# Row products with an operand in PSUM and every second low part on GpSimd, in a hybrid attention and expert block

## The chip, the cores and the metric

One core of a Trainium2 chip runs the whole kernel. The metric is device time in microseconds, median of three runs.

## The reference

One residual layer over 512 tokens of width 2048, and a last RMSNorm. The first half is a mixer of two attentions (eight heads each), gated and merged. The change lies in the second half, a product-key retrieval of single-neuron experts:

```python
def peer_ffn(h, w_query, sub_keys, expert_u, expert_v):       # h: RMSNorm(x), 512 x 2048
    q = (ht @ w_query).reshape(n_tok, 8, 2, 128)
    scores = einsum('thpc,hpnc->thpn', q, sub_keys)           # 128 keys per half
    # top 16 of each half, top 16 of the 16x16 sums: 128 experts of 16384 per token
    gates = softmax(top_score)
    act = gelu(einsum('thkd,td->thk', expert_u[ids], x))
    return einsum('thk,thkd->td', gates * act, expert_v[ids])
```

All arrays are float32, and the output must agree to nearly that.

## The kernel before, in words

Activations lie with the features on partitions (16 blocks of 128) and tokens along the row. To keep precision at the fast rate, each matmul operand is split into a rounded high part and the low part that is left, and `mm3` (L115 to L118) multiplies high with high, high with low and low with high. Weights come through `wload` (L95): a block of 128x2048 in two halves of 128x1024 (512 KB each, on SP's queue); ScalarE makes the high part (`wh`, L108), VectorE subtracts it for the low part (`wl`, L109). There are three buffers each of `wh` and `wl`, and four of the raw halves.

The expert stage begins at L487. Query projections, keys and scores give each token its 128 experts (`choose`, L653: tops, indices, gates). Then two ways of computing the experts run side by side:

- Densely, for the first 352 tokens (`TD`): for each of 128 blocks of 128 experts, `expert_up` (L532) multiplies all of them with the tokens (`psu`), VectorE scales (L536), ScalarE applies gelu. 54 of these blocks (`NS`) are done early: 40 beside `choose`, five after each head, and 14 beside the scatter (L777 to L793), which spreads the gates into a dense table in DRAM (`gsp`, stored from GpSimd's queue). Their activations are kept in DRAM (`gact_sp`). The rest are computed between the product groups.
- By gathered rows, for the last 160 tokens: GpSimd gathers for each of them the row of one expert (128 rows of 2048, 1 MB, `row_of`, L557), and VectorE multiplies it: an up product with the token's own row (L568, L577) that sums into one number, or a down product that adds the weighted row to an accumulator (L586, L597). There are 320 of them: 128 and 32 up, 128 and 32 down, in the list `todo` (L613). `pace` (L549) takes them from the list as the dense work goes on: 0.8 for each block in the early stage, then at a rate that empties the list at the end. The 32 tokens of the second kind stand four times side by side, so that 32 rounds serve their 128 experts. `token_rows` (L514) turns token columns into rows through TensorE transposes; `back` and `back_b` (L599, L606) turn the sums back.

The dense products come in 16 groups of eight expert blocks (L828). `weigh` (L808) brings the next activation, loads a group's gates when its first block comes (`gg`, which lies in columns of h2 that the dense part doesn't use, in one copy), multiplies (L817), and splits the result into high (L820) and low (L821): `wg`, nine buffers. Activations pass through four buffers (`gl`). Then 16 accumulations of 24 matmuls (`psy`), each added to the residual by VectorE (L841).

PSUM: two banks `pu`, two `py`, two `psx` and two `pg` in the first part of the stage; the last four give way to two `py2`, so that `psy` turns over four banks. Row buffers: two in the early stage, a third (`ex`) for every third row from the product groups on.

The order within each engine's queue is not the order of the program text: a scheduler fills each queue with what is ready first by its own estimate, earlier text first among the ready, and each queue then runs strictly in order. `tc.issue_after` holds an instruction behind a named one on its engine.

Of the kernel before, what the change touches and what calls it, by code (L numbers as in the profile page):

```python
# [13 lines left out]
ALU = mybir.AluOpType  # L14
# [36 lines left out]
def block_kernel(ctx, tc, xT, gains, w_vf, bf, w_qk, w_v, w_g, w_br, w_o, w_q, keysT, uT, vP, expert_u, expert_v, outT):  # L51
# [450 lines left out]
    rows_p = pool("rows", 1)  # L502
    accg = acc[:, :, T - P:]
    def norm2():
        ps = py.tile([P, T], F32, tag="py", name="psn2")
        nc.tensor.matmul(ps, ones, rstd, start=True, stop=True)
        rsqrt(rstd, ps, [gl.tile([P, T], F32, tag="gl", name="rs2") for i in range(3)])
        pt = py.tile([P, NT, P], F32, tag="py", name="psrt")
        for t in range(NT):
            nc.tensor.transpose(pt[:, t], rstd[:, t * P:(t + 1) * P], ident)  # L510
        for t in range(NT):
            nc.vector.tensor_copy(rstd_t[:, t:t + 1], pt[:, t, 0:1])

    def token_rows(cols, dst, x_dst=None):  # L514

        for j in range(0, KC, 4):
            if x_dst is not None:
                ps = py.tile([P, 4, P], F32, tag="py", name="psxg")
                for i in range(4):
                    nc.tensor.transpose(ps[:, i], cols(j + i), ident)  # L520
            ph = py.tile([P, 4, P], F32, tag="py", name="pshg")
            for i in range(4):
                tmp = gl.tile([P, P], F32, tag="gl", name="tmp")
                src = cols(j + i)
                nc.vector.tensor_scalar(tmp if len(src.shape) == 2 else tmp.rearrange("p (g m) -> p g m", m=MB), src,
                                        g_sb[:, KC + j + i:KC + j + i + 1], None, op0=ALU.mult)
                nc.tensor.transpose(ph[:, i], tmp, ident)
            if x_dst is not None:
                nc.scalar.activation(x_dst[:, j:j + 4], ps, AF.Copy)
            nc.scalar.activation(dst[:, j:j + 4], ph, AF.Copy)  # L530
# [15 lines left out]
    accb = h2g  # L546
    count, extra = [0], []
# [9 lines left out]
    def row_of(table, ids, i):  # L557
        count[0] += 1
        third = extra and count[0] % 3 == 0
        row = (extra[0] if third else rows_p).tile([P, KC, P], F32, tag="row", bufs=1 if third else 2, name="row")  # L560
        nc.gpsimd.indirect_dma_start(out=row.rearrange("p k q -> p (k q)"), out_offset=None, in_=table,  # L561
                                     in_offset=bass.IndirectOffsetOnAxis(ap=ids[:, i:i + 1], axis=0))
        return row

    def gather_up(i, after):
        row = row_of(expert_u, idx, i)
        with tc.issue_after(after):
            nc.vector.scalar_tensor_tensor(row, row, rstd_t[:, NT - 1:NT], h2g, op0=ALU.mult, op1=ALU.mult,  # L568
                                           accum_out=gact[:, i:i + 1])

    def rows_b(i, after):
        token_rows(lambda k: acc[:, k, TD:TD + MB].unsqueeze(1).to_broadcast([P, GB, MB]), h2g)

    def gather_up_b(i, after):
        row = row_of(expert_u, idx_b, i)
        with tc.issue_after(after):
            nc.vector.scalar_tensor_tensor(row, row, rstd_b, h2g, op0=ALU.mult, op1=ALU.mult,  # L577
                                           accum_out=gact_b[:, i:i + 1])

    def gather_down(i, after):  # L580
# [3 lines left out]
        row = row_of(expert_v, idx, i)  # L584
        with tc.issue_after(after):
            nc.vector.scalar_tensor_tensor(accg, row, gact[:, i:i + 1], accg, op0=ALU.mult, op1=ALU.add)  # L586

    def gather_down_b(i, after):
# [3 lines left out]
        row = row_of(expert_v, idx_b, i)  # L592
        with tc.issue_after(after):
            if i == 0:
                nc.vector.tensor_scalar(accb, row, gact_b[:, :1], None, op0=ALU.mult)
            else:
                nc.vector.scalar_tensor_tensor(accb, row, gact_b[:, i:i + 1], accb, op0=ALU.mult, op1=ALU.add)  # L597
# [8 lines left out]
    def back_b(i, after):  # L606
        for j in range(0, KC, 4):
            ps = py.tile([P, 4, MB], F32, tag="py", name="psbackb")
            for i in range(4):
                nc.tensor.matmul(ps[:, i], accb[:, j + i], sel_b, start=True, stop=True)  # L610
# [4 lines left out]
    todo += [(gather_down_b, i) for i in range(SB)] + [(lambda i, after: None, 0), (back, 0), (back_b, 0)]  # L615
# [12 lines left out]
    with ExitStack() as s1:  # L628
# [3 lines left out]
        psx = pool("psx", 2, space=PSUM, cm=s1)  # L632
        pg = pool("pg", 2, space=PSUM, cm=s1)
# [83 lines left out]
        for h in range(NH):  # L717
            sc = []
            sv = se.tile([P, 2, HT, NK], F32, tag="sv", name="sv")
            for p in range(2):  # L720
# [3 lines left out]
                if b == 3:  # L724
                    token_rows(lambda k: acc[:, k, T - P:], h2g, accg)
# [6 lines left out]
                ps = psx.tile([P, NT, NK], F32, tag="psx", name="pss")  # L732
# [16 lines left out]
        ps = psx.tile([P, T], F32, tag="psx", name="psrep")  # L749
# [18 lines left out]
        for n, src in enumerate((ia, ib, gt)):  # L768
            ps = psx.tile([P, ND, P], F32, tag="psx", name="pstr")
# [7 lines left out]
        for tb in range(TD // TB):  # L777
            st = se.tile([P, NK, TB], F32, tag="st", name="st")
            for t4 in range(0, TB, 4):
# [4 lines left out]
                ps = pg.tile([P, 4, NK], F32, tag="pg", name="psgt")  # L784
# [11 lines left out]
    extra.append(ex)  # L796
# [7 lines left out]


    ahead = []

    def weigh(n):  # L808
# [14 lines left out]

    ws = [weigh(0)]
    assert len(started) == NS
    rate[0] = len(todo) / (2 * NK - NS - 8)
    py2 = pool("py2", 2, space=PSUM)
    for grp in range(NG):  # L828
        while len(ws) < GC:
            ws.append(weigh(grp * GC + len(ws)))  # L830
        for jb in range(KC // JJ):
            w = wload(vP[grp, jb])
            for jj in range(JJ):
                j = jb * JJ + jj
                ps = (py, py2)[j % 2].tile([P, T], F32, tag="py", name="psy")
# [7 lines left out]
        ws = []  # L843
# [4 lines left out]
    fin = [rows_p.tile([P, 4, T], F32, tag="row", bufs=2, name="fin") for i in range(2)]  # L848
# [78 lines left out]
```

## Time and profile before

| | us |
|---|---|
| median of 3 runs (3779.3 to 3790.0) | 3787.84 |
| profiled execution | 3782.03 |
| its span | 3780.3 |

| 40 slices of 94.5 us | busy tenths of VectorE |
|---|---|
| slices 1 to 14 (attention, mixer, output) | 3 to 5 |
| slices 15 to 17 (query projection) | 4, 6, 7 |
| slices 18 to 40 (experts) | 5 to 9, mostly 8 |

The profile is one execution. Busy times of matmuls overlap, so a busy TensorE is not one at its peak: the number of matmuls in a stretch says more. GpSimd's busy time counts gathers only for as long as it writes their descriptors; the transfer comes after.

### The profile page before, as it was taken

Reading aid. Unit: us, or ns where it says so; the run is one execution under the profiler, and the core shown is the slowest. Engines: PE = TensorE matmul, PEld = TensorE weight load, DVE = VectorE, ACT = ScalarE, POOL = GpSimd, SP = SyncE. Lnnn points to the kernel's source line nnn. Section 1 sums busy time; section 2 is a strip of 40 time slices with the busy share of each in tenths; the row PEclk is TensorE's granted clock in tenths of the full one; section 3 lists DMA queues with packets and bytes.
Section 4 is the critical chain, followed back from the end, with each engine's and each line's share of the span. In section 5 each row is a group of like instructions: output and inputs, shape, how many; then the busy total and the mean of one; then the engine's idle time right before and its main releaser. Section 6 shows DMA issues by size and latency. Waiting matters only on the chain.

```text
span 3780.3 us, 52236 instructions
## 1 busy us (share of the span) xinstructions
PE 3676.0 (97%) x20745; PEld 3384.4 (90%) x20745; DVE 2640.2 (70%) x4067; ACT 1291.3 (34%) x1808; POOL 515.2 (14%) x432
## 2 busy tenths in 40 slices
PE   8999999999999999999999898999999999999997
PEld 7888888888887878799999798999999999999997
DVE  5333445444555346799699888988888888888885
ACT  4334222232223223344355332333333333333333
POOL 0000000000000000011211122222222222222220
PEclk9999999999999999999999999999999999999999
DMA  4222222222224233376867899998999989999983
GB/s 141 80 78 77 98 95 95 89 87 84 85 95 138 95 100 101 128 267 251 294 229 264 288 336 333 352 334 326 333 336 348 345 324 349 340 343 344 332 306 112
DMA packets 233701, 827.26 MB, mean 219 GB/s; under 512 B 21736, under 2 KB 82664, under 8 KB 189680
## 3 DMA queue, kind: packets, MB, share of 16 engines
q1 hardware_dynamic: 174032, 450.30, 34.5%
q0 software_dynamic: 49920, 360.74, 24.8%
q10 hardware_dynamic: 9504, 12.88, 0.9%
q8 instruction: 163, 2.67, 0.3%
q14 instruction: 82, 0.67, 0.1%
HBM read 784.72 MB, written 39.11 MB: 218 GB/s over the span
## 4 chain that ended last, share of the span: by engine, by line
PE 81%; DVE 9%; DMA 5%; issue 3%; ACT 1%; SPq 0%; POOL 0%; DVEq 0%; POOLq 0%; ACTq 0%
PE psy L118 7%; PE psy L117 7%; PE psy L116 7%; PE psu L118 6%; PE psu L116 6%; PE psu L117 6%; PE psg L118 3%; PE psg L117 3%; PE psq L118 3%; PE psg L116 3%; PE psq L117 3%; PE psq L116 3%; DVE wl L109 2%; DVE ab L787 2%; PE psk L118 2%
## 5 line engine op out<-in xcount | busy, mean ns | idle before, releaser
L108 ACT ACTIVATE wh<-wr 128x1024 fp32r<-128x1024 f32 x768 | 813.6, 1061 | 1933.4 <-PE psy L117 581.0
L109 DVE TENSOR_TENSOR wl<-wr,wh 128x1024 fp32r<-128x1024 f32 x768 | 935.5, 1221 | 504.4 <-ACT wh L108 500.5
L116 PE MATMUL psy<-wg,wh 128*128 128x352 f32 x2048 | 668.6, 327 | 26.6 <-ACT wg L820 25.8
L117 PE MATMUL psy<-wg,wh 128*128 128x352 f32 x2048 | 672.0, 328 | 8.7 <-DVE wg L821 8.7
L118 PE MATMUL psu<-h,wl 128*128 128x352 f32 x2048 | 666.7, 326 | 12.8 <-DVE wl L109 12.5
L118 PE MATMUL psy<-wg,wl 128*128 128x352 f32 x2048 | 669.8, 328 | 8.4 <-DVE wl L109 8.3
L116 PE MATMUL psu<-h,wh 128*128 128x352 f32 x2048 | 666.6, 325 | 4.0 <-DVE gl L536 2.9
L117 PE MATMUL psu<-h,wh 128*128 128x352 f32 x2048 | 662.8, 324 | 0.0
L116 PEld LDWEIGHTS psy<-wg,wh 128*128 128x128 f32 x2048 | 391.1, 191 | 29.0 <-ACT wg L820 27.6
L118 PEld LDWEIGHTS psu<-h,wl 128*128 128x128 f32 x2048 | 385.5, 188 | 18.9 <-DVE wl L109 18.7
L117 PEld LDWEIGHTS psy<-wg,wh 128*128 128x128 f32 x2048 | 391.0, 191 | 11.0 <-DVE wg L821 10.9
L118 PEld LDWEIGHTS psy<-wg,wl 128*128 128x128 f32 x2048 | 391.0, 191 | 10.0 <-DVE wl L109 9.9
L116 PEld LDWEIGHTS psu<-h,wh 128*128 128x128 f32 x2048 | 386.6, 189 | 5.0 <-issue 3.2
L117 PEld LDWEIGHTS psu<-h,wh 128*128 128x128 f32 x2048 | 386.9, 189 | 0.0
L561 POOL DMA_INDIRECT row<-eu,idx x128 | 192.4, 1503 | 901.5 <-DVE row L568 606.4
L568 DVE SCALAR_TENSOR_TENSOR row<-row,rstd_t,h2g 128x2048 f32<-128x2048 f32 x128 | 300.1, 2345 | 6.5 <-DMA row<-eu,idx 6.5
L586 DVE SCALAR_TENSOR_TENSOR acc<-row,gact,acc 128x2048 f32<-128x2048 f32 x128 | 300.1, 2345 | 1.9 <-DMA row<-ev,idx 1.9
L561 POOL DMA_INDIRECT row<-ev,idx x128 | 182.2, 1424 | 508.0 <-DVE acc L586 478.1
L116 PE MATMUL psq<-h,wh 128*128 128x512 f32 x512 | 204.5, 399 | 8.8 <-ACT wh L108 8.8
L117 PE MATMUL psq<-h,wh 128*128 128x512 f32 x512 | 205.6, 401 | 1.5 <-DVE h L167 1.4
L118 PE MATMUL psq<-h,wl 128*128 128x512 f32 x512 | 204.6, 400 | 0.1
L118 PE MATMUL psg<-h,wl 128*128 128x512 f32 x512 | 203.3, 397 | 0.0
(311 smaller groups left out, 5513.7 us busy)
## 6 DMA issues: line engine op xcount, KB each, us to landing
wr<-uT SPq DMA_DIRECT2D x256, 512.0 KB
wr<-vP SPq DMA_DIRECT2D x256, 512.0 KB
wr<-w_qk SPq DMA_DIRECT2D x64, 512.0 KB
wr<-w_g SPq DMA_DIRECT2D x64, 512.0 KB
gsp<-st POOLq DMA_DIRECT2D x22, 1024.0 KB
wr<-w_br SPq DMA_DIRECT2D x32, 512.0 KB
wr<-w_o SPq DMA_DIRECT2D x32, 512.0 KB
wr<-w_q SPq DMA_DIRECT2D x32, 512.0 KB
```

The source lines that it names most:

```text
L108: nc.scalar.activation(hi, raw, AF.Copy)
L109: ins = nc.vector.tensor_tensor(lo, raw, hi.bitcast(F32), op=ALU.subtract)
L116: nc.tensor.matmul(ps, wh, ah, start=start, stop=False)
L117: nc.tensor.matmul(ps, wh, al, start=False, stop=False)
L118: nc.tensor.matmul(ps, wl, ah, start=False, stop=stop)
L561: nc.gpsimd.indirect_dma_start(out=row.rearrange("p k q -> p (k q)"), out_offset=None, in_=table, in_offset=bass.IndirectOffsetOnAxis(ap=i ...
L568: nc.vector.scalar_tensor_tensor(row, row, rstd_t[:, NT - 1:NT], h2g, op0=ALU.mult, op1=ALU.mult, accum_out=gact[:, i:i + 1])
L586: nc.vector.scalar_tensor_tensor(accg, row, gact[:, i:i + 1], accg, op0=ALU.mult, op1=ALU.add)
L787: nc.vector.tensor_scalar(ab[0][:, i], i128, tr[0][:, t:t + 1], tr[2][:, t:t + 1], op0=ALU.is_equal, op1=ALU.mult)
```

## The change

- `wload`: from the expert stage on, the low part of the second half of each block is subtracted on GpSimd.
- The operand that a row product reads or accumulates into lies in PSUM: one tile of four banks (`pr`), which holds in turn norm2's work, the token rows, and the sums. `token_rows` transposes into it without a copy, and no longer turns the residual itself. The down products start from the first weighted row, and `back` adds the finished sums to the residual; ScalarE copies them out of PSUM (`sums`). `back` now comes before the down products of the second kind.
- Three row buffers in one pool throughout.
- PSUM: `pu` two banks, `px` two banks for all else (scores, scatter, `psy`, backs), `pr` four.
- The gates of the next group are asked for after the second weight block of a group, its first activation is weighed after the seventh.

```diff
@@ wload
-            ins = nc.vector.tensor_tensor(lo, raw, hi.bitcast(F32), op=ALU.subtract)
+            second = more and s == 1
+            ins = (nc.gpsimd if second else nc.vector).tensor_tensor(lo, raw, hi.bitcast(F32), op=ALU.subtract)
@@ pools
-    py = pool("py", 2, space=PSUM)
+    px = pool("px", 2, space=PSUM)
+    pr = pool("pr", 1, space=PSUM)
-    h2g = gpool.tile([P, KC, P], F32, name="h2g")
-    rows_p = pool("rows", 1)
-    accg = acc[:, :, T - P:]
+    rows_p = pool("rows", 3)
+    held = [None]
+    def hold(name):
+        held[0] = pr.tile([P, KC, P], F32, tag="pr", name=name)
+        return held[0]
@@ token_rows
-    def token_rows(cols, dst, x_dst=None):
...
+    def token_rows(cols, name):
+        dst = hold(name)
+        for j in range(KC):
+            tmp = gl.tile([P, P], F32, tag="gl", name="tmp")
+            src = cols(j)
+            nc.vector.tensor_scalar(tmp if len(src.shape) == 2 else tmp.rearrange("p (g m) -> p g m", m=MB), src,
+                                    g_sb[:, KC + j:KC + j + 1], None, op0=ALU.mult)
+            nc.tensor.transpose(dst[:, j], tmp, ident)
@@ row products
-            nc.vector.scalar_tensor_tensor(row, row, rstd_t[:, NT - 1:NT], h2g, op0=ALU.mult, op1=ALU.mult,
+            nc.vector.scalar_tensor_tensor(row, row, rstd_t[:, NT - 1:NT], held[0], op0=ALU.mult, op1=ALU.mult,
                                            accum_out=gact[:, i:i + 1])
...
+    def add_row(row, g, i, ins):
+        with tc.issue_after(ins):
+            if i == 0:
+                nc.vector.tensor_scalar(hold("accg"), row, g[:, :1], None, op0=ALU.mult)
+            else:
+                nc.vector.scalar_tensor_tensor(held[0], row, g[:, i:i + 1], held[0], op0=ALU.mult, op1=ALU.add)
...
+    def sums():
+        s = rows_p.tile([P, KC, P], F32, tag="row", name="sums")
+        for j in range(0, KC, 4):
+            nc.scalar.activation(s[:, j:j + 4], held[0][:, j:j + 4], AF.Copy)
+        return s
     def back(i, after):
+        s = sums()
         for j in range(0, KC, 4):
-            ps = py.tile([P, 4, P], F32, tag="py", name="psback")
+            ps = px.tile([P, 4, P], F32, tag="px", name="psback")
             for i in range(4):
-                nc.tensor.transpose(ps[:, i], accg[:, j + i], ident)
-            nc.scalar.activation(accg[:, j:j + 4], ps, AF.Copy)
+                nc.tensor.transpose(ps[:, i], s[:, j + i], ident)
+            nc.vector.tensor_tensor(acc[:, j:j + 4, T - P:], acc[:, j:j + 4, T - P:], ps, op=ALU.add)
...
-    todo += [(gather_down_b, i) for i in range(SB)] + [(lambda i, after: None, 0), (back, 0), (back_b, 0)]
+    todo += [(back, 0)] + [(gather_down_b, i) for i in range(SB)] + [(back_b, 0)]
@@ product groups
+    def gates(grp):
+        for b in range(0, TD // TB, 8):
+            e = min(b + 8, TD // TB)
+            nc.sync.dma_start(gg[:, b:e], gsp[:, b:e, grp * GC:(grp + 1) * GC])
...
-        if n % GC == 0:
-            for b in range(0, TD // TB, 8):
-                e = min(b + 8, TD // TB)
-                nc.sync.dma_start(gg[:, b:e], gsp[:, b:e, n:n + GC])
...
+    gates(0)
     ws = [weigh(0)]
-    py2 = pool("py2", 2, space=PSUM)
     for grp in range(NG):
+        first = []
...
             w = wload(vP[grp, jb])
+            if grp + 1 < NG and jb == 1:
+                gates(grp + 1)
+            if grp + 1 < NG and jb == KC // JJ - 2:
+                first.append(weigh((grp + 1) * GC))
...
-                ps = (py, py2)[j % 2].tile([P, T], F32, tag="py", name="psy")
+                ps = px.tile([P, T], F32, tag="px", name="psy")
...
-        ws = []
+        ws = first
```

## Rows read from the trace of the kernel before

**Rows 1.** The page's first part: busy us, share of the span, instructions.
```profile
PE 3676.0 (97%) x20745; PEld 3384.4 (90%) x20745; DVE 2640.2 (70%) x4067; ACT 1291.3 (34%) x1808; POOL 515.2 (14%) x432
```

**Rows 2.** Windows: stretch, us, busy of PE, PEld, DVE, ACT, POOL, clock, DMA.
```profile
1590.00:1905.00 315.00, 303.13 (x1842) 299.30 (x1841) 272.76 (x730) 137.93 (x223) 49.41 (x33) 0.98 0.74 264
...
1800.00:1905.00 105.00, 105.00 (x656) 105.00 (x655) 69.17 (x79) 37.51 (x46) 18.79 (x11) 1.00 0.77 277
...
1905.00:2117.00 212.00, 198.55 (x1393) 191.34 (x1392) 209.97 (x509) 124.64 (x134) 26.86 (x33) 0.99 0.72 259
...
2130.00:2543.00 413.00, 389.57 (x2309) 385.17 (x2310) 357.05 (x432) 124.33 (x149) 106.68 (x69) 0.96 0.92 334
...
2800.00:3000.00 200.00, 200.00 (x1241) 200.00 (x1240) 174.72 (x159) 65.70 (x76) 52.72 (x37) 1.00 0.93 347
3000.00:3758.00 758.00, 750.67 (x4644) 749.24 (x4642) 624.42 (x572) 253.64 (x306) 174.85 (x123) 1.00 0.84 311
```

**Rows 3.** Waits of TensorE, whole run: us in total, times, longest us.
```profile
PE psy L116 <- ACT wg L820: 25.8, 6, 12.1
PE psu L118 <- DVE wl L109: 12.5, 15, 2.6
...
PE psy L117 <- DVE wg L821: 8.7, 5, 3.6
PE psy L118 <- DVE wl L109: 8.3, 4, 2.9
PE psgt L789 <- DVE ab L787: 7.3, 11, 2.1
```

**Rows 4.** Groups by line: count, busy us, mean ns, idle before and its releaser.
```profile
L109 DVE TENSOR_TENSOR wl<-wr,wh 128x1024 fp32r<-128x1024 f32 x768 | 935.5, 1221 | 504.4 <-ACT wh L108 500.5 <-issue 0.8
...
L586 DVE SCALAR_TENSOR_TENSOR acc<-row,gact,acc 128x2048 f32<-128x2048 f32 x128 | 300.1, 2345 | 1.9 <-DMA row<-ev,idx 1.9
...
L536 DVE TENSOR_TENSOR gl<-psu,rstd 128x352 f32<-128x352 f32 x128 | 66.4, 518 | 72.1 <-PE psu L118 71.9
L817 DVE TENSOR_TENSOR gl<-gl,h 128x352 f32<-128x352 f32 x128 | 64.8, 519 | 71.5 <-DMA h<-gsp 49.5 <-DMA gl<-gact_sp 21.9
L821 DVE TENSOR_TENSOR wg<-gl,wg 128x352 fp32r<-128x352 f32 x128 | 64.1, 518 | 4.6 <-ACT wg L820 4.6
...
L520 PE MATMUL psxg<-ident,acc 128*128 128x128 f32 x16 | 2.5, 279 | 0.0
```

**Rows 5.** Timeline of a steady product group: start us, us, engine, line, [idle <-releaser].
```profile
2839.04 1.06 ACT L108 ACTIVATE wh<-wr 128x1024 fp32r<-128x1024 f32 x1 [2.29 <-PE psy L117]
...
2841.85 1.22 DVE L109 TENSOR_TENSOR wl<-wr,wh 128x1024 fp32r<-128x1024 f32 x1
...
2842.21 1.68 POOL L561 DMA_INDIRECT row<-ev,idx  x1 [6.10 <-DVE acc L586]
...
2842.93 1.06 ACT L108 ACTIVATE wh<-wr 128x1024 fp32r<-128x1024 f32 x1 [2.83 <-PE psy L117]
2843.05 0.52 DVE L841 TENSOR_TENSOR acc<-acc,psy 128x352 f32<-128x352 f32 x1
```

**Rows 6.** Timeline of a group border, SP's queue and VectorE.
```profile
2195.53 2.06 SPq L802 DMA_DIRECT2D gl<-gact_sp  x4
...
2202.83 0.53 DVE L817 TENSOR_TENSOR gl<-gl,h 128x352 f32<-128x352 f32 x1 [4.45 <-DMA gl<-gact_sp]
...
2205.26 0.37 SPq L815 DMA_DIRECT2D h<-gsp  x1
```

**Rows 7.** Timeline of a later border, SP's queue and VectorE.
```profile
3066.20 8.32 SPq L815 DMA_DIRECT2D h<-gsp  x3
...
3084.55 0.53 DVE L817 TENSOR_TENSOR gl<-gl,h 128x352 f32<-128x352 f32 x1 [8.78 <-DMA h<-gsp]
```

**Rows 8.** Timeline of the end: VectorE beside GpSimd.
```profile
3766.23 7.99 DVE L876 SCALAR_TENSOR_TENSOR acc<-acc,g_sb,psr 128x512 f32<-128x512 f32 x12 [2.80 <-ACT rstd L871]
3766.29 4.94 POOL L874 TENSOR_TENSOR acc<-acc,rstd 128x512 f32<-128x512 f32 x4 [102.74 <-ACT rstd L871]
```

More of the change, by code (lines that the diff above doesn't have):

```diff
@@ L501, in block_kernel @@
     sel_b = gpool.tile([P, MB], F32, name="sel_b")
-    rows_p = pool("rows", 1)
-    accg = acc[:, :, T - P:]
+    rows_p = pool("rows", 3)
[3 more added lines that the diff above has]
+        return held[0]
     def norm2():
-        ps = py.tile([P, T], F32, tag="py", name="psn2")
+        both = hold("psn2")
+        ps = both[:, :NT].rearrange("p t q -> p (t q)")
         nc.tensor.matmul(ps, ones, rstd, start=True, stop=True)
         rsqrt(rstd, ps, [gl.tile([P, T], F32, tag="gl", name="rs2") for i in range(3)])
-        pt = py.tile([P, NT, P], F32, tag="py", name="psrt")
+        pt = both[:, NT:2 * NT]
         for t in range(NT):
@@ L512, in norm2 @@
             nc.vector.tensor_copy(rstd_t[:, t:t + 1], pt[:, t, 0:1])
-    def token_rows(cols, dst, x_dst=None):
[L516 to L530, printed above, removed]
+    def token_rows(cols, name):
[6 more added lines that the diff above has]
+            nc.tensor.transpose(dst[:, j], tmp, ident)
     def expert_up(c, pace=None):
@@ L545, in block_kernel @@
     gg = gg.rearrange("p b (c t) -> p b c t", t=TB)
-    accb = h2g
-    count, extra = [0], []
     def pace(after, units):
@@ L557, in row_of @@
     def row_of(table, ids, i):
-        count[0] += 1
-        third = extra and count[0] % 3 == 0
-        row = (extra[0] if third else rows_p).tile([P, KC, P], F32, tag="row", bufs=1 if third else 2, name="row")
+        row = rows_p.tile([P, KC, P], F32, tag="row", name="row")
         nc.gpsimd.indirect_dma_start(out=row.rearrange("p k q -> p (k q)"), out_offset=None, in_=table,
@@ L583, in gather_down @@
             nc.vector.tensor_tensor(gact, gact, ggate, op=ALU.mult)
-        row = row_of(expert_v, idx, i)
-        with tc.issue_after(after):
-            nc.vector.scalar_tensor_tensor(accg, row, gact[:, i:i + 1], accg, op0=ALU.mult, op1=ALU.add)
+        add_row(row_of(expert_v, idx, i), gact, i, after)
     def gather_down_b(i, after):
@@ L591, in gather_down_b @@
             nc.vector.tensor_tensor(gact_b, gact_b, ggate_b, op=ALU.mult)
[L592 to L597, printed above, removed]
+        add_row(row_of(expert_v, idx_b, i), gact_b, i, after)
+    def sums():
[3 more added lines that the diff above has]
+        return s
     def back(i, after):
+        s = sums()
         for j in range(0, KC, 4):
-            ps = py.tile([P, 4, P], F32, tag="py", name="psback")
+            ps = px.tile([P, 4, P], F32, tag="px", name="psback")
             for i in range(4):
-                nc.tensor.transpose(ps[:, i], accg[:, j + i], ident)
-            nc.scalar.activation(accg[:, j:j + 4], ps, AF.Copy)
+                nc.tensor.transpose(ps[:, i], s[:, j + i], ident)
+            nc.vector.tensor_tensor(acc[:, j:j + 4, T - P:], acc[:, j:j + 4, T - P:], ps, op=ALU.add)
     def back_b(i, after):
+        s = sums()
         for j in range(0, KC, 4):
-            ps = py.tile([P, 4, MB], F32, tag="py", name="psbackb")
+            ps = px.tile([P, 4, MB], F32, tag="px", name="psbackb")
             for i in range(4):
-                nc.tensor.matmul(ps[:, i], accb[:, j + i], sel_b, start=True, stop=True)
+                nc.tensor.matmul(ps[:, i], s[:, j + i], sel_b, start=True, stop=True)
             nc.vector.tensor_tensor(acc[:, j:j + 4, TD:TD + MB], acc[:, j:j + 4, TD:TD + MB], ps, op=ALU.add)
@@ L731, in block_kernel @@
                 nc.sync.dma_start(kt, keysT[b])
-                ps = psx.tile([P, NT, NK], F32, tag="psx", name="pss")
+                ps = px.tile([P, NT, NK], F32, tag="px", name="pss")
                 for t in range(NT):
@@ L748, in block_kernel @@
         nc.vector.tensor_copy(spread, ident[:, P - MB:].unsqueeze(1).to_broadcast([P, GB, MB]))
-        ps = psx.tile([P, T], F32, tag="psx", name="psrep")
+        ps = px.tile([P, T], F32, tag="px", name="psrep")
         nc.tensor.matmul(ps[:, :2 * HK + 2], spread.rearrange("p g m -> p (g m)"), rep, start=True, stop=True)
@@ L768, in block_kernel @@
         for n, src in enumerate((ia, ib, gt)):
-            ps = psx.tile([P, ND, P], F32, tag="psx", name="pstr")
+            ps = px.tile([P, ND, P], F32, tag="px", name="pstr")
             for t in range(ND):
@@ L783, in block_kernel @@
                                         tr[1][:, tk].unsqueeze(2).to_broadcast([P, 4, NK]), op=ALU.is_equal)
-                ps = pg.tile([P, 4, NK], F32, tag="pg", name="psgt")
+                ps = px.tile([P, 4, NK], F32, tag="px", name="psgt")
                 for i in range(4):
@@ L842, in block_kernel @@
                 pace(add, 1.0 / JJ)
-        ws = []
+        ws = first
     while todo:
         pace(add, 1.0)
-    fin = [rows_p.tile([P, 4, T], F32, tag="row", bufs=2, name="fin") for i in range(2)]
+    fin = [rows_p.tile([P, 4, T], F32, tag="row", name="fin") for i in range(2)]
     ssq = fin[0][:, 0]
```

9 lines of the change are left out of this document (3 added, 6 removed).

## The prediction

> **What bounds the kernel now.** I read the busy shares first [rows 1]: TensorE is busy 97% of the 3780.3 us span, VectorE 70%, so no edit that only makes VectorE lighter can give more than TensorE's own holes. Next the stretches [rows 2], because the diff touches only what comes after the output projection. In 2800 to 3000 us TensorE issues 1241 matmuls in 200 us, 0.1612 us each, and is never idle: that is the pace of the expert products undisturbed. Held against it, 2130 to 2543 us (413 us, room for 2562) shows 2309: 253 x 0.1612 = 40.8 us lost, idle time and the lower clock after it (mean granted clock 0.96) together. 3000 to 3758 us lacks 58 of 4702, 9.3 us. In 1590 to 1905 us 1842 matmuls need 296.9 of 315 us, 18 us lost; in the scatter (1905 to 2117 us) TensorE is idle 13.5 us while VectorE is busy 209.97 of 212 us. So the whole stage holds some 80 us that an edit could win, 2%, in four places with different causes.
>
> The waits of TensorE [rows 3] name them: 25.8 us for the high part of the expert weights (ACT wg, 6 times), 12.5 us in the early experts for a low part from VectorE, 8.7 us for wg's low part, 8.3 us for a weight's low part in the products, 7.3 us for the scatter's operands.
>
> The timeline of a border [rows 6] shows what is behind the largest: the last activations of the next group are asked for at 2195.53 (when the low parts of wg let go of the four gelu buffers), and VectorE waits until 2202.83 for them; TensorE's stall is that transfer, 7.3 us. The gates of the group after (h<-gsp) are issued at 2205.26, right behind the last multiplication that reads the old ones. So they are already asked for at the first moment at which their buffer is free. [rows 7] shows the other kind: gates issued at 3066.20, VectorE standing 8.78 us in order on the first multiplication of the next group until 3084.55, the low part of the weights queued behind it.
>
> **The change part by part.**
>
> *Every second low part on GpSimd.* It takes 1.22 us off VectorE [rows 4] for each weight block of two halves, and gives GpSimd a two-operand subtraction of 128x1024. The trace has GpSimd's multiplication of 128x512: four in 4.94 us, 1.235 us each [rows 8]. Bounds: 1.24 us (as if length cost nothing) to 5 us (twice the doubled row, if the rounded output or VectorE's reads hold it); I take 2.5 us, the row doubled, because on VectorE the rounded output costs nothing beside its length [rows 4]: 1.22 us for 1024 elements, 0.52 us for 352. Is it in time? In the steady stretch [rows 5] the high part starts at 2839.04, when TensorE is through with the half three before. That half is needed two groups of 24 matmuls later, 2 x 3.87 = 7.74 us, so 6.7 us after the high part is done at 2840.10. On VectorE the low part ended at 2843.07. On GpSimd it ends at 2842.6, or at 2844.3 with one gather of 1.68 us ahead of it: still 2.5 us early. GpSimd's load in 2800 to 3000 us [rows 2]: 52.7 us for gathers and 26 x 2.5 = 65 us, 59%. VectorE's: 174.7 - 26 x 1.22 = 143 us, 72%. There TensorE is already full, so this part gives 0 in the products' steady stretch. It counts where VectorE is late.
>
> Early experts, 1590 to 1905 us: by the code 40 experts, so 40 low parts leave VectorE, 49 us of its time. TensorE's waits for low parts are 12.5 us over this stretch and the scatter; I take 6 us here. Scatter: 14 experts and the first product block, 15 low parts x 1.22 = 18 us off an engine that is full; TensorE's idle 13.5 us is the cap. But GpSimd's queue is in order, and the stores of the scatter and the gathers that wait for a row buffer stand in it ahead of the low part. I take 7 us gained, between 13 gained and 20 lost (the rival below). Borders: VectorE's share of the waits is 8.7 + 8.3 us; less work ahead of wg's low parts lets the gelu buffers go sooner, by at most one low part (1.22 us) at each of ten borders; I take 6 us. Against it, GpSimd's low part stands behind a gather whose buffer is late: 0 to 20 us, I take 5 us, since the 2.5 us left above cover most.
>
> *Operands of the row products in PSUM.* 320 products, 2.345 us each [rows 4]. VectorE takes 0.518 us with an operand in PSUM (gl<-psu,rstd) and 0.519 us with both in SBUF (gl<-gl,h), so the up products keep their time. No row shows VectorE writing PSUM, as the down products now do; from the twelve of 128x512 with a PSUM operand in 7.99 us [rows 8] four would be 2.66 us, so 2.27 (four of them overlapped like the whole) to 2.66 us; I take 2.35. Even at 2.66 the 160 down products add 50 us to an engine that goes from 87 to 72% busy: 0. The transposes of x into the accumulator go: 16 of TensorE, 2.5 us [rows 4], at 1415 us where nothing else holds it: 2.5 us won. What comes new (eight ACT copies out of PSUM, four VectorE additions of 128x512) lies beside full TensorE stretches; the one new point where TensorE waits in order, the transposes of the first token block in mid-run, costs 0 to 4 us, I take 1.
>
> *PSUM shared anew.* The products turn over two banks in place of four. In [rows 5] the half's last high product is done at 2842.93 (it lets the next high part start); the addition that empties its bank starts at 2843.05 and takes 0.52 us; with two banks it is needed again 3.87 us after the group's end. If VectorE does a row product and a delayed low part first (2.35 + 1.22 + 2.5 us) the addition is 2.2 us too late. In the steady stretch that sequence does not occur, since the slots with VectorE's low part and with GpSimd's alternate. 0, at worst 10 us lost.
>
> *Gates and the first weights asked for mid-group.* The queues are filled by what is ready first, and [rows 6, 7] show the gates leaving right behind the last multiplication that frees their buffer, and the first multiplication of the next group already ahead in VectorE's queue. A request written later in the program cannot leave earlier. The buffers that decide the border (four of gelu, nine of wg) are unchanged. I take 0; it would be 35 us at best, below. *Three row buffers* in the early stage instead of two: gathers run further ahead; VectorE waits little for rows now, 0.
>
> Sum: -2.5 - 6 - 7 - 6 + 5 + 1 = -15.5 us. The profiled execution took 3782.03 us (1.7 us around the span); the median shown is 3787.84 us, 5.8 us above it. Against the median: 3787.84 - 15.5 = 3772 us.
>
> **Rivals.**
>
> *1. GpSimd and VectorE hold one another up (slower).* Place: 1590 to 2117 us, where VectorE is full and works on operands in SBUF. If a GpSimd low part keeps VectorE's next two-operand instruction waiting for its own length, each costs up to 2.5 us to save 1.22 us: +1.28 us. Scatter: 15 x 1.28 = 19 us, and all of it on the path; early experts: 40 x 1.28 = 51 us, of which 36 us are covered (VectorE is busy only 69 of 105 us in 1800 to 1905 us); the borders, where VectorE's weighing is all in SBUF, 10 x 1 us. Together 19 + 15 + 10 = 44 us, less the 2.5 us of the transposes and some half of the 19 us of relief counted above: +30 us, 3818 us. It decides from 1.22 us of hold per low part. For it: VectorE's rows there are mostly SBUF operands. Against: GpSimd's 1.235 us ran beside VectorE's additions without a mark [rows 8], but those had one operand in PSUM, so the row does not settle it. The Trainium skill speaks for this rival: SBUF — State Buffer, "Who interferes with whom", says that a VectorE instruction with two SBUF inputs and a GpSimd one that reads SBUF exclude each other, the later one standing until the other is done. By the same rule the row products, with one operand moved to PSUM, are out of it; no run here shows either.
>
> *2. The borders close.* If the mid-group request does bring gates and first weights in time (a new order of VectorE's queue could do it), the stalls of [rows 6, 7] go: of 40.8 + 9.3 us some 30 more than counted. 3772 - 30 = 3742 us. For it: both chains end in a transfer. Against: the gelu transfers, not the gates, end last in [rows 6], and their buffers are the same.
>
> *3. The relief does not reach TensorE.* Low parts come from GpSimd as late as from VectorE, because the gather ahead waits for VectorE's row product anyway; only the transposes count: 3785 us.
>
> **How the numbers follow.** Forecast 0.42, rival 1 0.27, rival 2 0.16, rival 3 0.15. Range: down to rival 2, up to rival 1, 3738 to 3820 us; the forecast's own 3758 to 3786. Within 0.3% (about what can be told from no change) is 3776.5 to 3799.2: faster 0.31 + 0.16 = 0.47; same 0.11 + 0.13 = 0.24; slower 0.27 + 0.02 = 0.29.
>
> **What would show it.** Right: GpSimd low parts of about 2.5 us, VectorE near 72% in the products, the scatter shorter by some 7 us, 2130 to 2543 us still some 35 us above its pace. Row products at 2.35 us with either operand in PSUM. Wrong: low parts on GpSimd above 4 us or VectorE's own low parts stretched beyond 1.22 us (rival 1); group borders without stalls (rival 2); TensorE waiting for GpSimd's low part in many steady groups, which none of the cases has.

## The result, and the profile after

The changed kernel takes 3868.71 us (median of 4 runs, 3866.38 to 3870.19); beside it the kernel before takes 3787.38. The ratio is 1.0218, with a 95% interval of 1.020 to 1.0236. So the change costs 2.2%, some 82 us, where the forecast had it 15.5 us faster and the range ended at 3820. The profiled execution has a span of 3865.9 us, 85.6 us above that of before.

The page's first part, to be held against [rows 1] (busy us, share of the span, instructions):

```profile
PE 3695.7 (96%) x20729; PEld 3392.2 (88%) x20729; DVE 2522.0 (65%) x3799; ACT 1289.4 (33%) x1806; POOL 1097.7 (28%) x704
```

VectorE did become lighter, 70 to 65%, and GpSimd took the work over, 14 to 28%. The engine that was relieved is not the one that sets the end. The same five long stretches as in [rows 2] (stretch, us, busy time and instructions of PE, PEld, DVE, ACT and POOL, TensorE's clock, DMA share, GB/s):

```profile
1590.00:1905.00 315.00, 286.21 (x1709) 281.31 (x1708) 251.45 (x684) 136.57 (x220) 128.99 (x69) 0.96 0.69 249
1905.00:2117.00 212.00, 193.06 (x1308) 186.47 (x1307) 189.66 (x420) 110.89 (x120) 60.77 (x45) 0.98 0.65 237
2130.00:2543.00 413.00, 364.30 (x2166) 359.17 (x2165) 306.88 (x395) 123.78 (x147) 187.92 (x108) 0.94 0.87 315
2800.00:3000.00 200.00, 195.41 (x1201) 193.03 (x1200) 155.55 (x139) 65.51 (x80) 100.88 (x61) 1.00 0.88 327
3000.00:3758.00 758.00, 735.19 (x4496) 726.32 (x4496) 578.89 (x465) 238.85 (x281) 384.69 (x228) 1.00 0.89 327
```

Every stretch issues fewer matmuls: 1709 for 1842 in the first, 1201 for 1241 in the one that was full before. The stretches are fixed in time while the work in them has moved later, so I read each as a pace. The first product starts at 2169.7 us for 2130.2 (39.6 us late); the rest of the loss, 46 us, comes after it. TensorE's longest waits, against [rows 3]:

```profile
PE psu L119 <- DVE wl L110: 45.5, 38, 5.0
PE psy L117 <- ACT wg L821: 32.2, 8, 14.1
PE psgt L791 <- DVE ab L789: 21.7, 16, 2.8
PE psy L118 <- DVE wg L822: 12.2, 3, 8.0
...
PE psu L119 <- POOL wl L110: 2.8, 5, 1.2
```

TensorE hardly waits for GpSimd's low parts (2.8 us). It waits for the low parts that stayed on VectorE, in the up products of the experts: 45.5 us where it was 12.5. VectorE has less to do and delivers later. One place in the middle of the run shows how; VectorE first, then GpSimd in the same time (start us, us):

```profile
2848.24 2.34 DVE L573 SCALAR_TENSOR_TENSOR row<-row,rstd_b,h2g 128x2048 f32<-128x2048 f32 x1
...
2850.50 2.67 DVE L818 TENSOR_TENSOR gl<-gl,h 128x352 f32<-128x352 f32 x1
2853.10 1.21 DVE L110 TENSOR_TENSOR wl<-wr,wh 128x1024 fp32r<-128x1024 f32 x1
```

```profile
2850.41 2.39 POOL L110 TENSOR_TENSOR wl<-wr,wh 128x1024 fp32r<-128x1024 f32 x1 [0.87 <-ACT wh L108]
```

TensorE around the end of that low part:

```profile
2853.19 0.32 PE L118 MATMUL psu<-h,wh 128*128 128x352 f32 x1
2854.37 0.44 PE L119 MATMUL psu<-h,wl 128*128 128x352 f32 x1 [0.86 <-DVE wl L110]
```

The weighing (L818) starts 0.09 us after GpSimd's subtraction, and its record runs for 2.67 us, to 0.37 us after the end of that subtraction. Its usual length is 0.52 us. The low part behind it starts 2.15 us late, and the matmul that needs it starts 1.18 us after the matmul before it, where 0.16 us is the pace. (The expectations of runs 3 and 11 give stalls of this kind as 1.33 us; from matmul to matmul they are mostly 1.18.) The row product ahead of the weighing, which now reads one operand from PSUM, kept its 2.34 us. How far the instructions are stretched over the whole run (count, then min/median/max in ns):

```profile
L818 DVE TENSOR_TENSOR gl<-gl,h x128: 507/520/3266, 2168.6 to 3781.6; 128x352 f32<-128x352 f32 x128
L822 DVE TENSOR_TENSOR wg<-gl,wg x128: 507/522/3290, 2169.9 to 3782.7; 128x352 fp32r<-128x352 f32 x128
```

```profile
L789 DVE TENSOR_SCALAR ab<-i,ia,gt x352: 328/335/2796, 1932.6 to 2154.7; 128x128 f32<-128x128 f32 x176
```

The medians are as before; the longest are the usual length plus 2.5 to 2.8 us, about one GpSimd subtraction. Adding up what stands above the median, I get some 180 us of VectorE's time from 1290 us on, some 118 of them from the first product on. By start times the picture is sharp. Of the instructions that VectorE began more than 0.2 us before the end of a GpSimd subtraction, all 65 of the weighing (multiplication L818 and low part L822) were held, and none of 18 row products and none of 23 additions, which have one operand in PSUM:

```profile
L847 DVE TENSOR_TENSOR acc<-acc,psy x256: 503/520/523, 2178.5 to 3843.8; 128x352 f32<-128x352 f32 x128
```

Two things that the prediction had to size without a row of their own came out as estimated (groups by line: count, busy us, mean ns, idle before):

```profile
L564 DVE SCALAR_TENSOR_TENSOR row<-row,rstd_t,h2g 128x2048 f32<-128x2048 f32 x128 | 299.2, 2338 | 0.2 <-DMA row<-eu,idx 0.2
L581 DVE SCALAR_TENSOR_TENSOR accg<-row,gact,accg 128x2048 f32<-128x2048 f32 x127 | 298.0, 2347 | 3.9 <-DMA row<-ev,idx 3.9
```

```profile
L110 POOL TENSOR_TENSOR wl<-wr,wh 128x1024 fp32r<-128x1024 f32 x272 | 656.1, 2412 | 651.6 <-ACT wh L108 597.2 <-DMA h<-gsp 22.0 <-DVE acc L847 10.2
```

### The profile page after: what moved, and what is told of

It is laid out like the page before. It is cut to its first block, busy times and chain, and to the rows that moved or that the text cites. A ratio compares the mean times of both kernels' runs of the same rounds, so it can differ in the third digit from the quotient of the medians.

```text
span 3865.9 us, 52751 instructions
## 1 busy us (share of the span) xinstructions
PE 3695.7 (96%) x20729; PEld 3392.2 (88%) x20729; DVE 2522.0 (65%) x3799; ACT 1289.4 (33%) x1806; POOL 1097.7 (28%) x704
## 5 line engine op out<-in xcount | busy, mean ns | idle before, releaser
L110 DVE TENSOR_TENSOR wl<-wr,wh 128x1024 fp32r<-128x1024 f32 x496 | 614.1, 1238 | 486.6 <-ACT wh L108 484.5
L110 POOL TENSOR_TENSOR wl<-wr,wh 128x1024 fp32r<-128x1024 f32 x272 | 656.1, 2412 | 651.6 <-ACT wh L108 597.2
L119 PE MATMUL psu<-h,wl 128*128 128x352 f32 x2048 | 672.4, 328 | 48.3 <-DVE wl L110 45.5
L117 PE MATMUL psy<-wg,wh 128*128 128x352 f32 x2048 | 668.4, 327 | 34.9 <-ACT wg L821 32.2
L118 PEld LDWEIGHTS psy<-wg,wh 128*128 128x128 f32 x2048 | 391.8, 191 | 13.6 <-DVE wg L822 13.6
L581 DVE SCALAR_TENSOR_TENSOR accg<-row,gact,accg 128x2048 f32<-128x2048 f32 x127 | 298.0, 2347 | 3.9 <-DMA row<-ev,idx 3.9
L557 POOL DMA_INDIRECT row<-eu,idx x128 | 165.3, 1291 | 283.5 <-DVE row L564 212.1
L847 DVE TENSOR_TENSOR acc<-acc,psy 128x352 f32<-128x352 f32 x256 | 132.5, 517 | 170.1 <-PE psy L119 169.7
L557 POOL DMA_INDIRECT row<-ev,idx x128 | 152.8, 1194 | 225.5 <-DVE accg L581 200.6
```

Source lines behind the costliest of these rows:

```text
L110: ins = (nc.gpsimd if second else nc.vector).tensor_tensor(lo, raw, hi.bitcast(F32), op=ALU.subtract)
L117: nc.tensor.matmul(ps, wh, ah, start=start, stop=False)
L118: nc.tensor.matmul(ps, wh, al, start=False, stop=False)
L119: nc.tensor.matmul(ps, wl, ah, start=False, stop=stop)
L581: nc.vector.scalar_tensor_tensor(held[0], row, g[:, i:i + 1], held[0], op0=ALU.mult, op1=ALU.add)
L847: add = nc.vector.tensor_tensor(acc[:, j, :TD], acc[:, j, :TD], ps[:, :TD], op=ALU.add)
```

## The experiments

Eleven kernels. Times are compared by the ratio to the kernel before, which ran beside each on the same chip; 0.001 of it is 3.8 us, and differences between two runs are worked out from their ratios. Four theories stood at the start: **L**, GpSimd's reading holds VectorE's two-operand instructions; **O**, the new order of the queues; **B**, the two banks of psy; and GpSimd's queue being late, which the 2.8 us above already spoke against.

**1. All low parts back on VectorE.**

```diff
-            second = more and s == 1
-            ins = (nc.gpsimd if second else nc.vector).tensor_tensor(lo, raw, hi.bitcast(F32), op=ALU.subtract)
+            ins = nc.vector.tensor_tensor(lo, raw, hi.bitcast(F32), op=ALU.subtract)
```

> The changed kernel with every low part of the weights back on VectorE; all the rest of the change stays. Theory L (while GpSimd's subtraction reads SBUF, VectorE's instructions with two SBUF operands stand for its length, some 180 us of stretch in the changed kernel's trace, and TensorE waits for the low parts held up behind them): no VectorE instruction is stretched any more, TensorE's waits for VectorE's low part fall from 45.5 us to 12 to 20, and the time comes back to 3785 us, give or take 15. Theory O (the new order of the queues: gates and a first weighing mid-group, one more up product within a group): the stretch goes but the time stays over 3840 us. Theory B (psy on two PSUM banks in place of four): the same, over 3840 us.

Measured: 3778.35 us, ratio 0.9989 (0.9976 to 1.0002). Against the changed kernel's 1.0218 that is 0.0229, 87 us (83.4 between the profiled spans), which the low parts on GpSimd alone cost. Theory L's range for the time holds it. The stretch is gone, and TensorE's wait for VectorE's low part is back to 8.9 us, below the 12 to 20 expected:

```profile
PE psy L116 <- DVE acc L846: 10.9, 4, 4.8
PE psu L118 <- DVE wl L109: 8.9, 10, 2.6
```

```profile
L821 DVE TENSOR_TENSOR wg<-gl,wg x128: 515/519/527, 2125.7 to 3697.7; 128x352 fp32r<-128x352 f32 x128
```

```profile
L788 DVE TENSOR_SCALAR ab<-i,ia,gt x352: 334/345/486, 1903.1 to 2110.9; 128x128 f32<-128x128 f32 x176
```

The early experts' stretch, to be held against the 1709 matmuls of the changed kernel:

```profile
1590.00:1905.00 315.00, 306.21 (x1888) 303.71 (x1887) 277.63 (x740) 139.23 (x227) 47.84 (x35) 0.99 0.76 274
```

**2. Only the low parts on GpSimd, in the kernel before.** The edit is that of run 1 the other way round.

> The kernel before with one edit only: the second low part of each weight pair on GpSimd. The row products keep both operands in SBUF. Theory L: the row products are held too, so that they are recorded at over 2.5 us in the mean in place of 2.35, and the time is above that of the changed kernel, 3870 to 3960 us. Theories O and B, which see the cost in what this kernel does not have: 3770 to 3800 us, as before.

Measured: 3916.47 us, ratio 1.0356 (1.0336 to 1.0377). Theory L's range holds it; with run 1, O and B are out as the main cause, for this kernel has neither. Its row products, both operands in SBUF, are held (min/median/max in ns):

```profile
L569 DVE SCALAR_TENSOR_TENSOR row<-row,rstd_t,h2g x128: 2328/2346/5078, 1600.8 to 2701.6; 128x2048 f32<-128x2048 f32 x128
```

```profile
L587 DVE SCALAR_TENSOR_TENSOR acc<-row,gact,acc x128: 2333/2346/5191, 2884.1 to 3616.6; 128x2048 f32<-128x2048 f32 x128
```

The means are 3.22 and 2.97 us; in the changed kernel they are 2.34 and 2.35. By start times, 58 of the 59 row products that began more than 0.2 us before the end of a subtraction were held here, none of 18 in the changed kernel. So moving one operand of the row products to PSUM does what it can do: it takes these 320 instructions out of the hold. It leaves the weighing and VectorE's other two-operand work in SBUF in it.

**3. The gates and the first weighing as before, the rest changed.**

```diff
+        if n % GC == 0:
+            gates(n // GC)
...
-            if grp + 1 < NG and jb == 1:
-                gates(grp + 1)
-            if grp + 1 < NG and jb == KC // JJ - 2:
-                first.append(weigh((grp + 1) * GC))
```

> The changed kernel with the request of the gates and the first weighing put back to where the kernel before has them; low parts on GpSimd and the new PSUM sharing stay. Theory L: within 10 us of the changed kernel's 3868.7, since the holding is as it was. Theory O: 30 us or more faster, down to 3835 or less, with the stalls of 1.33 us in the experts between groups gone.

Measured: 3891.64 us, ratio 1.0276 (1.0252 to 1.030). Theory O is out with the sign reversed: the new order gains 22 us (0.0058) in this kernel. Theory L's "within 10 us" missed that as well. Two of TensorE's waits are longer here than in the changed kernel, for the high part of the weighted activations (50.7 us for 32.2) and for the addition that empties a bank (13.4 for 2.8):

```profile
PE psy L117 <- ACT wg L823: 50.7, 10, 12.0
...
PE psy L117 <- DVE acc L844: 13.4, 5, 5.2
```

Run 4, and runs 5, 6 and 9 on the kernel before, follow it up.

**4. The PSUM sharing alone** (the edits of runs 1 and 3 together).

> The changed kernel with the low parts on VectorE and the gates and first weighing as before: what stays of the change is the PSUM sharing (row operands and sums in PSUM, psy over two banks, three row buffers, no transposes of x). Theory L: 3775 to 3795 us, about the kernel before, and within 10 us of the run with only the low parts put back. Theory B: over 3840 us. Theory O would have this one near the kernel before and the one with only the low parts put back well above it.

Measured: 3803.98 us, ratio 1.0052 (1.0035 to 1.0069). So the sharing by itself costs 20 us, between what L and B said, and against run 1 the mid-group requests are worth 24 us here too. A new wait stands in TensorE's list, for the addition that empties a psy bank:

```profile
PE psy L116 <- DVE acc L843: 22.1, 6, 4.6
PE psy L117 <- DVE wg L823: 13.9, 7, 3.8
```

In run 1 the same wait is 10.9 us. In this order the three parts make up the whole: +20 for the sharing, -24 for the requests, +87 for GpSimd, from the kernel before to the changed one.

**5. The mid-group requests alone, on the kernel before.** The edit of run 3 the other way round.

> The kernel before with one edit only: the gates asked for mid-group and the first weighing of the next group written into the group's last block but one. Putting this in was worth 23 us on the changed kernel (3868.7 against 3891.6) and 26 us on the one with only the low parts put back (3778.4 against 3804.0). Theory M (the order helps whatever the banks: the stalls at the borders go): 3757 to 3765 us here too. Theory N (it only wins back what the two banks of psy lose, since the steady stretch 2800 to 3000 us issues 1201 matmuls without it, 1236 with it and 1241 in the kernel before): 3778 to 3790 us.

Measured: 3785.67 us, ratio 1.0000 (0.9991 to 1.0009). As theory N had it, with four banks the requests are worth nothing. That elsewhere they only win back what two banks lose is argued and not shown: they are worth 22 and 24 us there, and run 6 finds 10 us lost to two banks alone.

**6. Two banks alone, on the kernel before.**

```diff
-                ps = (py, py2)[j % 2].tile([P, T], F32, tag="py", name="psy")
+                ps = py.tile([P, T], F32, tag="py", name="psy")
```

> The kernel before with one edit only: psy turns over two PSUM banks in place of four. Theory B (the 21 us that the PSUM sharing costs are TensorE's waits for the additions that empty a bank, 22.1 us in the run with the PSUM sharing alone): 3800 to 3815 us, with waits of psy for VectorE's addition of 15 to 30 us. Rival (the cost lies elsewhere in the sharing: sums in PSUM, copies, back in mid-run): 3780 to 3790 us.

Measured: 3793.95 us, ratio 1.0026 (1.0017 to 1.0036): 10 us, between the ranges of B and its rival, with a wait of psy for the addition of 13.0 us in three holes:

```profile
PE psy L116 <- DVE acc L841: 13.0, 3, 4.6
```

All three are at a border, and VectorE's timeline at one of them says why two banks don't cover it:

```profile
3090.70 0.53 DVE L817 TENSOR_TENSOR gl<-gl,h 128x352 f32<-128x352 f32 x1 [9.12 <-DMA h<-gsp]
3091.15 1.22 DVE L109 TENSOR_TENSOR wl<-wr,wh 128x1024 fp32r<-128x1024 f32 x1
3092.28 0.52 DVE L821 TENSOR_TENSOR wg<-gl,wg 128x352 fp32r<-128x352 f32 x1
3092.72 0.51 DVE L841 TENSOR_TENSOR acc<-acc,psy 128x352 f32<-128x352 f32 x1
```

VectorE stands 9.12 us, in order, on the gates of the next group; the addition comes third behind it. It is the standing of [rows 7]. Two banks hold two groups of 3.87 us, 7.74 together, less than the 9 us and the work ahead of the addition. The other two holes show the same, with 7.78 and 8.56 us on the gates. Run 4 has six such waits for three here; what else in the sharing makes the other three, and its other 10 us, these runs don't separate.

**7 and 8. GpSimd busy, but no part of the computation:** all low parts on VectorE, and after each second one GpSimd overwrites the raw tile, by a memset or by a copy onto itself.

```diff
+            if more and s == 1:
+                nc.gpsimd.memset(raw, 0.0)          # run 7
+                nc.gpsimd.tensor_copy(raw, raw)     # run 8, in its place
```

> The run with all low parts on VectorE (3778.4 us), and after each second low part a GpSimd memset of the same 128x1024 raw tile, which is no part of the computation: GpSimd is busy and in order, writes SBUF and reads none, and no TensorE operand waits for it. Theory L (it is the reading of SBUF on GpSimd that holds VectorE's instructions with two SBUF operands): additions and weighing are not stretched (weighing 0.52 us), at most the single-operand comparison of the scatter is; 3775 to 3795 us. Rival (any work of GpSimd in SBUF of that length holds VectorE, or the queue's occupancy is what costs): over 3820 us.

> The same place and tile, but a GpSimd copy of the raw tile onto itself in place of the memset: it reads SBUF as well as writes it, with the same buffers and waits. Theory L: the two-operand instructions of VectorE are stretched by up to the copy's length and the time is over 3840 us, more than the changed kernel's if the copy is as long as its subtraction, because VectorE also keeps all low parts. Rival (queue or buffers): the same time as with the memset, within 10 us.

Measured: 3800.54 us, ratio 1.0042 (1.0026 to 1.0057) with the memset, 3820.00, ratio 1.0088 (1.0072 to 1.0103) with the copy. Both expectations of time missed: the memset was 5 us above its range, the copy 20 us below. The copy is short, 1.12 us for 2.41, so the time cannot be compared with the changed kernel's; the tiles can. GpSimd's operation, then VectorE's low part and the scatter's comparison, in run 7:

```profile
L111 POOL MEMSET wr<- 128x1024 f32 x272 | 261.4, 961 | 631.1 <-DVE wl L109 437.8 <-issue 173.8 <-DVE rep L749 11.0
```

```profile
L109 DVE TENSOR_TENSOR wl<-wr,wh x768: 1200/1221/1259, 8.1 to 3764.4; 128x1024 fp32r<-128x1024 f32 x191, 128x1056 fp32r<-128x1056 f32 x1
```

```profile
L790 DVE TENSOR_SCALAR ab<-i,ia,gt x352: 328/336/1678, 1908.3 to 2122.5; 128x128 f32<-128x128 f32 x176
```

and in run 8:

```profile
L111 POOL COPY wr<-wr 128x1024 f32<-128x1024 f32 x272 | 305.2, 1122 | 626.5 <-DVE wl L109 437.6 <-issue 173.5 <-DVE rep L749 11.0
```

```profile
L109 DVE TENSOR_TENSOR wl<-wr,wh x768: 1194/1221/2605, 7.7 to 3784.9; 128x1024 fp32r<-128x1024 f32 x191, 128x1056 fp32r<-128x1056 f32 x1
```

```profile
L790 DVE TENSOR_SCALAR ab<-i,ia,gt x352: 327/335/1674, 1913.0 to 2132.4; 128x128 f32<-128x128 f32 x176
```

The same place, the same buffers, the same queue. Beside writes alone the two-operand subtraction never exceeds 1.26 us; beside an operation that also reads SBUF it reaches 2.61. By start times, none of the 55 low parts and weighing instructions that began beside a memset (more than 0.2 us before its end) was held, and 40 of 43 beside a copy. The comparison, with one tile as operand, is held by both. The rival of run 8, the same time with either, is out by 17 us (0.0046). That separates reading from occupying GpSimd, which is what theory L needed. It agrees with the Trainium skill, SBUF — State Buffer, "Who interferes with whom", which excludes two SBUF inputs on VectorE only against a GpSimd instruction that reads SBUF, and counts tensor_scalar among the operations that may take the shared ports also against writes. Of the 20 us (0.0053) by which the memset stands above run 1, 6.5 are in the scatter; the rest, before and after it, stays unexplained.

**9 and 10. The first weighing tied behind an addition,** so that VectorE does not stand on the gates; run 9 on the kernel of run 5 (four banks), run 10 on that of run 1 (two banks).

```diff
-                first.append(weigh((grp + 1) * GC))
+                first.append(weigh((grp + 1) * GC, add))
...
+        with tc.issue_after(after.ins) if after is not None else nullcontext():
             nc.vector.tensor_tensor(g.rearrange("p (b t) -> p b t", t=TB), ...
```

> The run with the gates asked for mid-group on the kernel before (3785.7 us), and the first weighing of a group tied behind the last addition written before it, so that VectorE doesn't stand on the gates with low parts and additions queued behind it. Theory G (that standing, 8.78 us at 3084 us in the kernel before, is what makes TensorE's late holes: five of 1.4 to 3.4 us after 2550 us, 11.6 us together): those holes go, 3770 to 3778 us. Rival (the holes are covered or come back, because the gelu buffers come free later): 3780 us or more.

> The same tie on the run with all low parts on VectorE (3778.4 us), which has psy on two banks: its late holes, 5.2, 3.3 and 3.4 us at 2573, 3076 and 3204 us, all stand at an addition behind a wait for gates. Theory G: 3760 to 3770 us, faster than both kernels. Rival: 3775 us or more.

Measured: 3783.96 us, ratio 1.0002 (0.9991 to 1.0013), and 3775.10 us, ratio 0.9975 (0.9962 to 0.9987). VectorE's standing on the gates after 2545 us, 38.2 us in the kernel before, is gone from both. With four banks it bought nothing, as the rival had it. With two banks the wait for the addition went from 10.9 to 1.1 us, but the time came out only 5 us below run 1 (0.0014), which is within the intervals of the two runs and less than the 8 to 18 us of theory G; the rival's 3775 us or more holds here too. Run 10 is 92 us faster than the changed kernel and 0.25% faster than the kernel before (0.13 to 0.38), the one version here whose interval lies below the kernel before.

**11. GpSimd's low parts in the products' blocks only,** 128 of the 272.

```diff
-    def wload(src, between=None, pace=None):
+    def wload(src, between=None, pace=None, gp=False):
...
-            second = more and s == 1
+            second = gp and s == 1
...
-            w = wload(vP[grp, jb])
+            w = wload(vP[grp, jb], gp=True)
```

> The changed kernel with GpSimd's low parts in the expert products' blocks only, 128 of the 272; the blocks of the up products (early experts, scatter, experts between groups) have both low parts on VectorE. Against the run with all on VectorE the changed kernel lost 29.5 us before the scatter, 13.6 in it and 39 after the first product. Theory L (what counts is whether VectorE then has two-SBUF instructions on the path; in the products' blocks its neighbours are row products and additions with a PSUM operand): the 43 us before the products go whole and most of the 39, 3780 to 3800 us, and the stalls of 1.33 us in the experts between groups are gone. Rival (a price per low part wherever it stands, 90 us / 272 = 0.33 us): 128 of them cost 42 us, 3820 us.

Measured: 3779.40 us, ratio 0.9990 (0.9978 to 1.0003), the time of run 1 and just under theory L's range. So the 87 us go with the 144 low parts in the blocks of the up products (GpSimd in these blocks alone was not run); a price per low part is out. The hold is still there: the weighing's low part (L822), mean 1059 ns in the changed kernel and 519 in run 1, is

```profile
L822 DVE TENSOR_TENSOR wg<-gl,wg 128x352 fp32r<-128x352 f32 x128 | 86.7, 691 | 8.3 <-ACT wg L821 7.6
```

but TensorE's waits for low parts are 12.4 us together, where run 1 has 9.2 and the changed kernel 52.1:

```profile
PE psu L119 <- DVE wl L110: 7.8, 8, 2.6
PE psy L119 <- DVE wl L110: 4.6, 5, 1.2
```

The likely reason, argued and not tested, is that in the products' blocks a held instruction meets VectorE with time to spare, and most of its neighbours have an operand in PSUM.

## Why the prediction was wrong

**The step that failed is the first of the change, "every second low part on GpSimd".** It put -6 for the early experts, -7 for the scatter, -6 for the borders against +5 for GpSimd's lateness, -14 together; against run 1 it measured +87. Rival 1 named the mechanism, its place and the rule, and had 0.27. It was set behind the forecast because [rows 8] showed GpSimd beside VectorE "without a mark", though the text itself said that an operand in PSUM kept that row from settling it. The row nearest in kind was not evidence on the point. The sign that was to tell rival 1, VectorE's own low parts above 1.22 us, hardly showed (1.24 us in the mean, 9 of 496 held): the hold fell on other instructions, and the low parts came late behind them. VectorE stood at 78% in 2800 to 3000 us, hold included, where 72 was forecast.

**Rival 1 was mis-sized too**, 3818 for 3869. It priced throughput: 1.28 us net for each low part, covered wherever VectorE had idle time. (Its sum also takes the relief off twice, since 1.28 is already net of the 1.22 us saved, and takes its cover of 36 us from 105 of the 315 us.) What the trace shows is delay in an ordered queue: one held instruction makes the low part behind it late by up to one GpSimd subtraction (2.41 us in the mean), and idle time elsewhere doesn't give that back. By place, in the profiled executions of the changed kernel and of run 1 (together 83.4 us):

- Early experts: 15 priced, 29.5 measured (the scatter's first product at 1933.2 for 1903.7 us). From 1590 to 1905 us the changed kernel issues 1709 matmuls in 286.21 us of busy time, 0.1675 us each at a clock of 0.96; run 1 has 1888 in 306.21, 0.1622 at 0.99. TensorE is idle 28.8 us for 8.8, 20 more, and 1709 x 0.0053 = 9 us go to the lower clock: in this stretch the granted clock is at 1.2 GHz, the lower of its two levels, for 23.9 us, in four pieces that each begin in or shortly after one of these holes, and in run 1 for 6.8 us. The cover of 36 us did not exist for work that has to be there at a time.
- Scatter: 19 priced, 13.6 measured (222.1 us between its first and last product for 208.5), while TensorE's waits for the held comparisons grew by 14.4 (21.7 for 7.3), which is the whole of it.
- After the first product: 10 priced at the borders, 39 measured (1673.7 for 1634.5 us to the last product). TensorE's waits for low parts in the experts between the groups, which no case had, make 22 of them (22.0 for 0.4); its waits for the high part of the weighted activations make 9 (18.0 for 9.1).

**Right:** GpSimd's subtraction at 2.5 us (2.41), the row products at 2.35 with either operand in PSUM (2.34 and 2.35), and nothing for the steady blocks of the products, where run 11 finds 128 low parts on GpSimd at no cost. Rival 1 was also right that the row products would be out of the hold.

**PSUM shared anew, "0, at worst 10 us lost":** two banks alone cost 10 us (run 6), the whole sharing 20 (run 4). The sequence looked for was a row product and a delayed low part ahead of the addition. The one that does it is VectorE standing on the gates, which was in [rows 7], read there only for the low part.

**Gates mid-group, "0":** right on the kernel before (run 5). In the changed kernel it is 22 us won (run 3), and there the waits for the weighted activations fall by 18.5 us and those for the addition by 10.6; how much of this is due to the two banks no run separates. It was judged on its own when it had to be judged on the kernel that the other edits make.

**The transposes, -2.5:** about 1.8 us won where they stood. From the last matmul of the output projection (pso) to the last of the scores (pss) it is 208.3 us in the kernel before (1371.8 to 1580.1) and 206.5 in run 1 (1373.3 to 1579.8); runs 5, 6 and 9, which still turn x, have 208.4 to 208.6, runs 4, 10 and 11 have 206.6 to 206.7. The changed kernel has 209.6: its low parts on GpSimd took it back. **Three row buffers, 0:** up to the scatter run 1 gains 7 us on the kernel before (1903.7 for 1910.8; nearly 9 counted from the last pso), at 1590 to 1905 us 1888 matmuls for 1842. It comes with the PSUM sharing, for run 4 has it too (1904.6); beyond the transposes, which part of it, no run tells.

**A misreading that moved no sum:** at the border of [rows 6] the 7.3 us are the transfer; TensorE's own wait there is 4.2 us.

## What to carry to other kernels

Before work moves to GpSimd, list which of VectorE's instructions beside it take two SBUF operands, and what stands behind them in the queue: a critical operand behind a held instruction comes late by up to the holder's length, however idle VectorE is on average. Moving one operand of the long instructions to PSUM frees just these; the short ones are held for as long. Edits that share a buffer's slack, here PSUM banks and the order at the borders, have to be judged together.

## What the runs showed of the hardware

A one-operand comparison of 128x128 (0.34 us) is held by GpSimd as a two-operand subtraction is, to 2.80 us in the changed kernel, and it is held to 1.68 us also beside a memset of 0.96 us, which leaves the subtraction at 1.22. Beside the memset one of the 88 comparisons that read two broadcast tiles took 1.33 us for 0.68, which looks like a two-operand instruction held by a write. It is not: its record begins inside that of a held one-operand comparison (1.58 us), 0.26 us before the memset starts, and both end at 2053.24 us, so it stood behind that comparison. Whether such comparisons of two broadcast tiles are held by reads these runs don't show, for none began more than 0.2 us before the end of a subtraction. GpSimd's subtraction is lengthened as well: it takes 2.66 us in the mean in run 2 (at most 4.48), where the row products have both operands in SBUF, and 2.41 in the changed kernel (at most 3.02).
